# Reading the conditioning rows of a one-core decoder layer in two passes instead of four

## The chip, the cores and the metric

The kernel runs on one core of a Trainium2 chip. The time is the device time of one execution in microseconds (us); for the kernel before it is the median of three runs. The profile is of one more execution.

## The reference, cut to what matters

One decoder layer on 256 tokens of width 2048: a SwiGLU feed-forward of width 5632, a mixer (retention beside a sliding-window attention, gated and merged), a second such feed-forward, and a final norm. All three sub-layers are conditioned by one vector `c`:

```python
c_act = jax.nn.silu(c)
mod = (c_act @ w_ada[l] + b_ada[l]).reshape(b, N_MOD, D_MODEL)      # N_MOD = 9
h = modulate(rms_norm(x, norm_ffn1[l]), mod[:, 0], mod[:, 1])
x = x + 0.5 * mod[:, 2][:, None, :] * swiglu(h, w_ffn1_gu[l], w_ffn1_down[l])
...                                                                 # mod 3, 4, 5 and 6, 7, 8 likewise
```

So `w_ada`, 2048 by 9 x 2048 in float32 (151 MB), is read once, and each of its columns is multiplied by the same vector and summed.

## The kernel before, in words

**Matrix products.** Tokens lie in two halves of 128. A weight block of 512 rows by 512 columns (1 MB) is loaded by `load` (line 346) on the queue of SyncE (SP) into one of four buffers named `raw`. It is used in two pieces of 256 rows. `split` (line 365) makes of each piece a high part `wh`, rounded by ScalarE (ACT, line 369), and a low part `wl`, the rest, by VectorE (DVE, line 371); three buffers each hold them. `products` (line 349) then runs three matmuls for each of two blocks of 128 rows and two halves of tokens: high by high (line 356), high by low (357), low by high (359), in all 12 a piece, on TensorE (PE). Where the activations lie whole in memory, they are split too, by lines 404 and 405. The sums lie in four accumulator banks named `pa`. After a down product, line 622 multiplies a bank by the gate row, which frees the bank, and line 623 adds that to `x_sb`.

**Conditioning.** `w_ada` is handed over turned, so that one row of 2048 floats per partition holds what 128 outputs need; nine outputs of 2048 values make 144 such rows of 1 MB. `ada_load` (line 214) loads a row, on SP's queue. `ada_pass` (line 219) multiplies a stretch of it by `cact`, which holds silu(c) on all partitions, and sums it on DVE into one column of `sums`; the page shows it as CUSTOM_DVE_ANT_0, followed by a read of the accumulator. `ada_end` (line 233) adds up the columns of `sums`, adds the bias and multiplies by the norm's gain; for a gate, `gate_out` (line 287) sends it out to memory, from where it returns as a row.

**The opening** (until about 300 us) reads the 32 rows of outputs 0 and 1, which the first norm needs. It states its own pass counts, most of them in `group` (line 975): eight rows are read in one pass of 2048 columns each, the other 24 in two of 1024.

**The rows behind it**, 112 for seven outputs, are read beside the matrix products. `conditioning` (line 261) is a generator that makes one pass a step, four of 512 columns a row (`AQ`). Ahead of a pass it loads every row that is needed up to `pace["ahead"]` steps later. `tick` (line 313) is called behind each piece of 12 matmuls; it adds `pace["rate"]` to `pace["due"]` and takes a step for each whole one. Rates are written by hand for each stage (steps a tick): 1.0 and then 160/117 in the first feed-forward, 0.95, 0.25 and 0.95 before, in and behind the softmax of the mixer, and 64/150 in the second feed-forward, which begins at `due` = -5. At first in the first feed-forward and in the mixer a row takes one of the four `raw` buffers (ahead 1 and 2); later, and in the second feed-forward, rows have a ring of two buffers of their own (`slot` or `rows_x`), with ahead = `AQ`, so that the next row is asked for at the first step of a row.

**Order.** SP's order is that of the program. The order on the other engines is dealt by a planner that takes, of the instructions whose inputs are there by its own estimate, the one that the program has first; only the opening and the stretch around each norm are written out by hand (no rows are read in the latter).

Of the kernel before, what the change touches and what calls it, by code (L numbers as in the profile page):

```python
# [77 lines left out]
def layer_kernel(  # L78
# [41 lines left out]
    def nm(s):  # L120
        uid[0] += 1
        return f"{s}_{uid[0]}"
# [82 lines left out]

    modc = one.tile([P, 9, KD], F32, tag="modc", name="modc")

    AQ = 4

    def ada_load(m, k, w, loads=1):  # L210
        src = w_ada[(m * KD + k) * P : (m * KD + k + 1) * P, :]
        for i in range(loads):
            at = slice(i * D // loads, (i + 1) * D // loads)
            nc.sync.dma_start(w[:, at], src[:, at])

    def ada_pass(k, w, sums, q, passes=AQ):

        at = slice(q * D // passes, (q + 1) * D // passes)
        nc.vector.tensor_tensor_reduce(  # L219
            out=w[:, at],  # L220
            in0=w[:, at],
            in1=cact[:, at],
            scale=1.0,
            scalar=0.0,
            op0=ALU.mult,
            op1=ALU.add,
            accum_out=sums[:, k, q : q + 1],
        )

    def ada_sums():  # L230
        return two.tile([P, KD, AQ], F32, tag="sums", name=nm("sums"))

    def ada_end(m, ks, sums, i=None, passes=AQ):

        dest = modc[:, m, ks]
        if passes > 1:
            nc.vector.tensor_reduce(
                out=dest, in_=sums[:, ks, :passes], axis=AX.X, op=ALU.add
            )
            nc.vector.tensor_add(dest, dest, bcols[:, m, ks])  # L240
        else:
            nc.vector.tensor_add(dest, sums[:, ks, 0], bcols[:, m, ks])
        if i is not None:
            nc.vector.tensor_mul(dest, dest, gains[:, i, ks])
# [5 lines left out]
    def two_rows(both=None):  # L250

        both = slot() if both is None else both
        turn = [both[:, :D], both[:, D:]]

        def place():
            turn.append(turn.pop(0))
            return turn[-1]

        return place

    def conditioning(outputs, place, behind):


        tiles = [(m, k) for m, _, _ in outputs for k in range(KD)]
        held = {}
        step = 0
        for m, gain, row in outputs:
            sums = ada_sums()
            for k in range(KD):
                for q in range(AQ):  # L270
                    for i in range(step // AQ, min((step + pace["ahead"]) // AQ + 1, len(tiles))):
                        if i not in held:
                            held[i] = place()
                            ada_load(*tiles[i], held[i])
                    if behind is not None and step < 2 * AQ:
                        with tc.issue_after(behind.ins):
                            ada_pass(k, held[step // AQ], sums, q)
                    else:
                        ada_pass(k, held[step // AQ], sums, q)
                    step += 1  # L280
                    if k == KD - 1 and q == AQ - 1:
                        ada_end(m, slice(0, KD), sums, gain)
                        if row is not None:
                            gate_out(m, row)
                    yield
# [18 lines left out]
    pace = {"steps": iter(()), "rate": 0.0, "due": 0.0, "behind": None}  # L304

    def set_pace(outputs, halves, place, ahead):
        assert next(pace["steps"], None) is None
        pace["steps"] = conditioning(outputs, place, pace["behind"])
        pace["rate"] = len(outputs) * KD * AQ / halves
        pace["due"] = 0.0  # L310
        pace["ahead"] = ahead
# [386 lines left out]
    def ffn_up(held, w, tiles, first, bg=None, turned=(), ahead=None):  # L698
        for ci in range(first, DFF // CH):
            bg = bg or gemm(held, w, [ci * CH])[0]  # L700
            bu = gemm(held, w, [DFF + ci * CH], ahead=ahead)[0]
            swiglu_up(bg, bu, tiles, ci, by_dma=ci in turned)
            bg = ahead = None
# [407 lines left out]
    for g, ks in enumerate(groups):  # L1111
# [5 lines left out]
        due = 0 if final else 2 * len(groups[g + 1])  # L1117
# [34 lines left out]
    gate = gate_row()  # L1152
    tiles.append(slot())
    row_ring.append(two_rows())
    pace["rate"] = (192 - 32) / 117
    pace["ahead"] = AQ
    ffn_up(held, gu, tiles, EARLY, turned=range(EARLY, DFF // CH))
    gate_in = gate_load(gate, 2)
# [7 lines left out]
        nc.gpsimd.dma_start(x_d[t], x_sb[:, t, :])  # L1166
    soft = one.tile([P, NT * D], F32, tag="x", name="soft")
    planes_of = one.tile([P, D], F32, tag="row", name="planes_of")
    RATE_SOFT, RATE_AFTER = 0.25, 0.95
    row_ring.clear()  # L1170
    set_pace([(7, 2, None), (6, None, None), (5, None, 1.0)], 192 / 0.95, place_row, 2)

    def rows_beside():

# [331 lines left out]
    gate = gate_row()  # L1506
    tiles = [slot() for _ in range(3)]
    set_pace([(8, None, 0.5)], 150, two_rows(), AQ)
    pace["due"] = -5.0
    ffn_up(held, w_ffn2_gu[0], tiles, 0, head, range(DFF // CH), ahead)  # L1510
    gf = one.tile([P, KD * S], F32, tag="hh", name="gf")[:, :D]
    spare = one.tile([P, 2, KD * P], F32R, tag="hl", name="spare")
# [108 lines left out]
```

## Time and profile before

| | |
|---|---|
| median of three runs | 2370.66 us (2369.91 to 2371.54) |
| the profiled execution | 2372.7 us |
| its span | 2370.9 us |
| granted clock of PE | 0.999 |
| moved by DMA | 627.87 MB, mean 265 GB/s |
| stages | opening to 300 us, first feed-forward to about 780, mixer to about 1660, second feed-forward to the end |

The span is the time from the first to the last instruction of the program. In views of groups a row gives line, engine, operation, output and inputs, shape and count, then busy time and mean length, then the engine's idle time just ahead of it and what ended it. In a row of windows, the stretch and its length are followed by the busy time and the number of instructions of PE, PE's weight loads (PEld), DVE, ACT and POOL, then PE's granted clock, the share of DMA time and GB/s; for the instructions of a single line only that engine's busy time is given. A row of an engine's order in time has the start, the length, the instruction, and in brackets the idle time before it with what ended it.

### The profile page before, as it was taken

What the parts mean: (1) busy time and instruction counts of PE and PEld (TensorE: products, weight loads), DVE (VectorE), ACT (ScalarE), POOL (GpSimd) and SP (SyncE); (2) the same over time, 40 slices, a digit from 0 to 9 for tenths busy, and PEclk for the clock granted to TensorE, in tenths of its full rate; (3) what the DMA queues carried; (4) which work ended last, traced back from release to release, by engine and by line L of the source; (5) the groups of instructions that cost most, each with busy time, mean ns of one, the idle gap of its engine ahead of it and who ended that gap; (6) DMA issues with size and microseconds to landing.
All of it is one profiled execution on the core that took longest, in us unless ns stands there. A gap on an engine that the chain in (4) does not pass through costs nothing.

```text
span 2370.9 us, 28254 instructions
## 1 busy us (share of the span) xinstructions
PE 2343.7 (99%) x10431; PEld 1917.9 (81%) x10431; DVE 1702.8 (72%) x2624; ACT 1312.8 (55%) x1782; POOL 9.2 (0%) x21
## 2 busy tenths in 40 slices
PE   8999999999999999999999999999999999999998
PEld 5888888888788877778888888888888888888886
DVE  7887799778877768976777776677655555555656
ACT  6544456455546568775556564466455455455544
POOL 0000000000000000000000000000000000000000
PEclk9999999999999999999999999999999999999999
DMA  9977789998866898876778787755677777766553
GB/s 384 360 290 265 274 284 345 386 319 333 317 256 231 281 274 235 251 224 244 269 274 293 299 303 277 289 195 188 240 240 247 252 242 250 245 220 203 193 198 124
DMA packets 186316, 627.87 MB, mean 265 GB/s; under 512 B 108801, under 2 KB 109185, under 8 KB 115649
## 3 DMA queue, kind: packets, MB, share of 16 engines
q1 hardware_dynamic: 183682, 615.05, 74.7%
q0 software_dynamic: 1600, 9.83, 1.0%
q8 instruction: 82, 1.34, 0.2%
q10 hardware_dynamic: 896, 1.19, 0.1%
q14 instruction: 56, 0.46, 0.1%
HBM read 597.16 MB, written 4.22 MB: 254 GB/s over the span
## 4 chain that ended last, share of the span: by engine, by line
PE 55%; DVE 1%; issue 0%; ACT 0%; DVEq 0%
PE pa L359 18%; PE pa L356 18%; PE pa L357 18%; DVE wl L371 0%; PE ps L1316 0%; PE pd L1416 0%; PE pd L1415 0%; PE pd L1414 0%; PE pd L1401 0%; PE ps L832 0%; DVE home L465 0%; DVE soft L1303 0%; DVE t L622 0%; PE pd L1404 0%; DVE hl L465 0%
## 5 line engine op out<-in xcount | busy, mean ns | idle before, releaser
L369 ACT CAST wh<-raw 128x1024 fp32r<-128x1024 f32 x792 | 831.1, 1052 | 916.8 <-PE pa L357 887.6
L371 DVE TENSOR_TENSOR wl<-raw,wh 128x1024 fp32r<-128x1024 f32 x792 | 962.5, 1224 | 518.9 <-ACT wh L369 517.3
L356 PE MATMUL pa<-wh,hh 128*128 128x512 f32 x2184 | 854.9, 391 | 2.2 <-ACT wh L369 2.2
L357 PE MATMUL pa<-wh,hl 128*128 128x512 f32 x2184 | 851.2, 390 | 0.0
L359 PE MATMUL pa<-wl,hh 128*128 128x512 f32 x2184 | 774.5, 392 | 3.4 <-DVE wl L371 3.0
L359 PEld LDWEIGHTS pa<-wl,hh 128*128 128x128 f32 x2184 | 408.3, 188 | 93.9 <-DVE wl L371 8.8
L356 PEld LDWEIGHTS pa<-wh,hh 128*128 128x128 f32 x2184 | 410.1, 188 | 91.0 <-ACT wh L369 3.9
L357 PEld LDWEIGHTS pa<-wh,hl 128*128 128x128 f32 x2184 | 410.3, 188 | 84.5 <-issue 0.2
L357 PE MATMUL pa<-wh,a 128*128 128x512 f32 x944 | 366.5, 390 | 0.0
L356 PE MATMUL pa<-wh,a 128*128 128x512 f32 x944 | 350.0, 390 | 1.8 <-DVE t L622 1.8
L359 PE MATMUL pa<-wl,a 128*128 128x512 f32 x944 | 348.5, 390 | 1.0 <-DVE wl L371 1.0
L219 DVE CUSTOM_DVE_ANT_0 slot<-slot,cact 128x512 f32<-128x512 f32 (+2 forms) x272 | 209.8, 822 | 21.9 <-DMA slot<-in_w_ada_dram 21.9
L356 PEld LDWEIGHTS pa<-wh,a 128*128 128x128 f32 x944 | 177.1, 188 | 39.0 <-DVE t L622 2.2
L359 PEld LDWEIGHTS pa<-wl,a 128*128 128x128 f32 x944 | 177.2, 188 | 38.6 <-DVE wl L371 2.1
L357 PEld LDWEIGHTS pa<-wh,a 128*128 128x128 f32 x944 | 177.3, 188 | 37.8 <-DVE a L405 1.1
L530 ACT COPY slot<-back 128x512 uint16<-128x512 uint16 x140 | 93.4, 766 | 0.0
L219 DVE CUSTOM_DVE_ANT_0 raw<-raw,cact 128x512 f32<-128x512 f32 (+1 forms) x108 | 70.9, 708 | 23.1 <-DMA raw<-in_w_ada_dram 23.1
L219 DVE CUSTOM_DVE_ANT_0 rows_x<-rows_x,cact 128x512 f32<-128x512 f32 x124 | 78.8, 689 | 7.5 <-DMA rows_x<-in_w_ada_dram 7.3
L405 DVE TENSOR_TENSOR a<-slot,a 128x512 fp32r<-128x512 f32 x118 | 80.8, 686 | 0.3 <-ACT a L404 0.2
L514 ACT COPY flat<-t 128x512 uint16<-128x512 uint16 x128 | 72.7, 617 | 4.5 <-DVE t L1389 2.6
L404 ACT CAST a<-slot 128x512 fp32r<-128x512 f32 x118 | 72.5, 615 | 0.1
L219 DVE DVE_READ_ACCUMULATOR2_ANT sums<- 128x1 f32 x504 | 42.4, 84 | 0.0
(228 smaller groups left out, 1169.6 us busy)
## 6 DMA issues: line engine op xcount, KB each, us to landing
raw<-in_w_ffn_gu_dram SPq DMA_DIRECT2D x160, 1024.0 KB, 5.3
raw<-in_w_in_dram SPq DMA_DIRECT2D x104, 1024.0 KB, 6.0
raw<-in_w_ffn_down_dram SPq DMA_DIRECT2D x88, 1024.0 KB, 4.8
slot<-in_w_ada_dram SPq DMA_DIRECT2D x83, 1024.0 KB, 7.0
rows_x<-in_w_ada_dram SPq DMA_DIRECT2D x31, 1024.0 KB, 7.0
raw<-in_w_ada_dram SPq DMA_DIRECT2D x26, 1024.0 KB, 5.6
raw<-in_w_swa_branch_dram SPq DMA_DIRECT2D x16, 1024.0 KB, 5.8
raw<-in_w_ret_branch_dram SPq DMA_DIRECT2D x16, 1024.0 KB, 5.8
```

The lines of the kernel that those rows point to most:

```text
L219: nc.vector.tensor_tensor_reduce(out=w[:, at], in0=w[:, at], in1=cact[:, at], scale=1.0, scalar=0.0, op0=ALU.mult, op1=ALU.add, accum_out= ...
L356: nc.tensor.matmul(ps, ah[:, j, ts], wh[:, j, :], start=first, stop=False)
L357: nc.tensor.matmul(ps, al[:, j, ts], wh[:, j, :], start=False, stop=False)
L359: nc.tensor.matmul(ps, ah[:, j, ts], wl[:, j, :], start=False, stop=last).ins
L369: cast.append(nc.scalar.copy(hi, src).ins)
L371: low.append(nc.vector.tensor_sub(lo, src, hi.bitcast(F32)).ins)
L404: nc.scalar.copy(hi, v)
L405: nc.vector.tensor_sub(lo, v, hi.bitcast(F32))
L514: nc.scalar.copy(planes[:, i, :], words(src)[:, :, i])
L530: nc.scalar.copy(into[:, :, :, i], held["turned"][:, i])
```

## The change

`AQ` becomes 2: each of the 112 rows is read in two passes of 1024 columns, and `sums` has two columns a row. A step is now half a row, so all rates in steps a tick are halved, and so is the negative start of the second feed-forward. `ahead` is 2 steps in place of 4 where it follows `AQ`, 1 in place of 2 at the mixer's beginning, and stays 1 in the first feed-forward. The opening is as it was.

```diff
-    AQ = 4
+    AQ = 2
...
-    pace["rate"] = (192 - 32) / 117
+    pace["rate"] = (96 - 16) / 117
     pace["ahead"] = AQ
...
-    RATE_SOFT, RATE_AFTER = 0.25, 0.95
+    RATE_SOFT, RATE_AFTER = 0.125, 0.475
     row_ring.clear()
-    set_pace([(7, 2, None), (6, None, None), (5, None, 1.0)], 192 / 0.95, place_row, 2)
+    set_pace([(7, 2, None), (6, None, None), (5, None, 1.0)], 192 / 0.95, place_row, 1)
...
     set_pace([(8, None, 0.5)], 150, two_rows(), AQ)
-    pace["due"] = -5.0
+    pace["due"] = -2.5
```

The generator that takes the steps is not changed:

```python
            for k in range(KD):
                for q in range(AQ):
                    for i in range(step // AQ, min((step + pace["ahead"]) // AQ + 1, len(tiles))):
                        if i not in held:
                            held[i] = place()
                            ada_load(*tiles[i], held[i])
```

## The prediction

> **What bounds the kernel now.** I read the page's busy times first, then the same busy times by stage, then what TensorE (PE) waited for between 300 and 2100 us.
>
> ```profile
> span 2370.9 us, 28254 instructions
> PE 2343.7 (99%) x10431; PEld 1917.9 (81%) x10431; DVE 1702.8 (72%) x2624; ACT 1312.8 (55%) x1782; POOL 9.2 (0%) x21
> ```
>
> ```profile
> 0.00:30.00 30.00, 20.98 (x42) 9.65 (x43) 19.98 (x47) 15.02 (x30) 1.79 (x7) 1.00 0.95 368
> 30.00:300.00 270.00, 267.96 (x1188) 219.11 (x1187) 223.44 (x305) 132.60 (x162) 0.00 (x0) 1.00 0.83 310
> 2340.00:2400.00 60.00, 21.78 (x97) 17.70 (x95) 14.25 (x32) 4.93 (x12) 0.00 (x0) 0.95 0.09 35
> ```
>
> ```profile
> 300.00:470.00 170.00, 169.59 (x761) 139.45 (x760) 147.39 (x263) 98.51 (x127) 2.09 (x4) 1.00 0.96 336
> 470.00:680.00 210.00, 207.83 (x915) 171.04 (x914) 181.39 (x339) 110.47 (x136) 0.00 (x0) 1.00 0.88 324
> 680.00:840.00 160.00, 160.00 (x723) 132.69 (x722) 113.67 (x176) 94.69 (x133) 1.08 (x2) 1.00 0.71 248
> 840.00:1140.00 300.00, 296.92 (x1413) 237.34 (x1412) 225.38 (x378) 206.10 (x366) 0.53 (x1) 1.00 0.81 243
> 1140.00:1580.00 440.00, 440.00 (x1952) 364.52 (x1951) 321.80 (x543) 244.17 (x315) 2.10 (x4) 1.00 0.78 281
> 1580.00:1660.00 80.00, 78.64 (x358) 63.79 (x357) 59.85 (x87) 50.82 (x86) 0.00 (x0) 1.00 0.51 185
> 1660.00:2100.00 440.00, 440.00 (x1942) 364.11 (x1941) 249.80 (x315) 224.15 (x263) 1.04 (x2) 1.00 0.73 244
> ```
>
> ```profile
> PE pa L359 <- DVE wl L371: 4.7, 7, 1.6
> PE pa L356 <- DVE t L622: 1.8, 1, 1.8
> PE pa L356 <- ACT wh L369: 0.5, 1, 0.5
> ```
>
> In the windows the first number after the stretch's length is PE's busy time. PE stands still for 9.0 us in the first 30 us and for about 9.1 us after 2340 (the span ends at 2370.9, so 30.9 less 21.78). The change touches neither end: the opening states its own pass counts, and the last conditioning row is read before 2100. Between 30 and 300 PE is idle 2.0 us. From 300 to 2100, where the changed rows lie (the first few are read shortly before 300), it is idle 0.41 + 2.17 + 0 + 3.08 + 0 + 1.36 + 0 = **7.0 us**, and the three waits (in total, how often, the longest) sum to the same 7.0: 6.5 of them for DVE. That is the ceiling of any gain, 0.3% of the span, unless a matmul itself became quicker.
>
> Could a matmul become quicker with a lighter VectorE (DVE)? Two stretches without PE idle time and with different DVE loads answer that:
>
> ```profile
> 1380.00:1440.00 60.00, 60.00 (x266) 49.56 (x265) 43.37 (x73) 34.47 (x42) 0.00 (x0) 1.00 0.88 312
> 1860.00:1920.00 60.00, 60.00 (x266) 49.70 (x265) 35.80 (x50) 32.93 (x40) 0.00 (x0) 1.00 0.74 248
> ```
>
> With DVE at 43 or at 36 of 60 us PE starts the same 266 matmuls, one each 0.226 us: no. [...]
>
> **The change part by part.** It replaces 448 passes of 512 columns (112 rows by four) by 224 of 1024, with one accumulator read behind each.
>
> ```profile
> L219 DVE CUSTOM_DVE_ANT_0 slot<-slot,cact 128x512 f32<-128x512 f32 x220 | 139.2, 688 | 7.0 <-DMA slot<-in_w_ada_dram 7.0
> L219 DVE CUSTOM_DVE_ANT_0 rows_x<-rows_x,cact 128x512 f32<-128x512 f32 x124 | 78.8, 689 | 7.5 <-DMA rows_x<-in_w_ada_dram 7.3
> L219 DVE CUSTOM_DVE_ANT_0 raw<-raw,cact 128x512 f32<-128x512 f32 x104 | 66.0, 688 | 23.1 <-DMA raw<-in_w_ada_dram 23.1
> L219 DVE CUSTOM_DVE_ANT_0 slot<-slot,cact 128x1024 f32<-128x1024 f32 x44 | 52.2, 1224 | 12.7 <-DMA slot<-in_w_ada_dram 12.7
> L219 DVE DVE_READ_ACCUMULATOR2_ANT sums<- 128x1 f32 x504 | 42.4, 84 | 0.0
> ```
>
> 220 + 124 + 104 = 448. The recorded lengths (688 and 1224 ns) overlap, so I take starts from DVE's order in time: one row of now, and two passes of 1024, which the opening already uses.
>
> ```profile
> 344.89 0.69 DVE L219 CUSTOM_DVE_ANT_0 raw<-raw,cact 128x512 f32<-128x512 f32 x1 [2.07 <-DMA raw<-in_w_ada_dram]
> ...
> 347.35 1.22 DVE L371 TENSOR_TENSOR wl<-raw,wh 128x1024 fp32r<-128x1024 f32 x1
> ```
>
> ```profile
> 161.63 1.23 DVE L219 CUSTOM_DVE_ANT_0 slot<-slot,cact 128x1024 f32<-128x1024 f32 x1 [2.51 <-DMA slot<-in_w_ada_dram]
> ...
> 163.93 2.36 DVE L371 TENSOR_TENSOR wl<-raw,wh 128x1024 fp32r<-128x1024 f32 x2
> ```
>
> Four passes occupy DVE for 347.35 - 344.89 = 2.46 us, two wide ones for 163.93 - 161.63 = 2.30 us. So a row costs **0.16 us less**, 112 rows 17.9 us of DVE time, from 1702.8 to about 1685. The row also shows that the four passes of a row run in one burst when the row has landed, whatever ticks they were dealt to; two wide ones will do the same.
>
> [...]
>
> What of the 0.16 us is on PE's path? DVE makes the low halves of the weights (wl, line 371), three in flight:
>
> ```profile
> 702.14 1.05 ACT L369 CAST wh<-raw 128x1024 fp32r<-128x1024 f32 x1 [1.66 <-PE pa L357]
> ...
> 703.23 1.23 DVE L371 TENSOR_TENSOR wl<-raw,wh 128x1024 fp32r<-128x1024 f32 x1 [1.49 <-ACT wh L369]
> ```
>
> In the steady state ScalarE (ACT) is idle until PE gives back a weight buffer, and 2.3 us later (702.14 to 704.46) both halves are ready. Two other pieces of 12 matmuls, 2 x 12 x 0.226 = 5.4 us, lie ahead of that one on PE: a **cushion of 3.1 us**. A burst of 2.46 us in front of a split fits into it; so does one of 2.30. What PE gains by the shorter burst is nothing there. If the cushion is gone, every microsecond of a burst is on PE's path. Two places show it, and two smaller ones (the burst at 344.89 above, in front of an 0.2 us wait, and a like one 22 us later):
>
> ```profile
> 635.85 0.69 DVE L219 CUSTOM_DVE_ANT_0 slot<-slot,cact 128x512 f32<-128x512 f32 x1
> ...
> 638.90 0.69 DVE L622 TENSOR_TENSOR t<-pa,row 128x512 f32<-128x512 f32 x1
> ```
>
> ```profile
> 851.10 0.69 DVE L219 CUSTOM_DVE_ANT_0 raw<-raw,cact 128x512 f32<-128x512 f32 x1 [4.20 <-DMA raw<-in_w_ada_dram]
> ...
> 854.15 3.50 DVE L371 TENSOR_TENSOR wl<-raw,wh 128x1024 fp32r<-128x1024 f32 x3
> ```
>
> At 638.90 the last multiply that frees an accumulator bank (L622) stands behind a burst; that is the 1.8 us wait of PE. At 851.10 DVE sits 4.2 us before a row that has not landed, then runs the burst, and the split behind it is late: the 1.6 us wait. Four such places, 0.16 us each: **-0.6 us**.
>
> **The order.** A pass that can't be cut for 1.15 us (half of 2.30) instead of 0.61 can hold a split or a bank's release 0.53 us longer. DVE's order is dealt by the planner, not written out, so this can fall either way: between -0.5 and +0.5 us at each of the four places, up to 2.1 us either way. I take zero.
>
> **The loads.** The queue of SyncE (SP) follows the program's order. A step is now twice as long in ticks, and with the row ring ("ahead" = AQ) the next row is asked for at a row's first step, which comes one old step later; with ahead 2 turned into 1 it is asked for at the last step, again one old step later. With ahead 1 in the first feed-forward nothing moves. Each weight load that was behind a row load in that stretch goes ahead of it. SP waited there at times for a pass to give a row's buffer back, with a weight load next in line:
>
> ```profile
> SPq L346 <- DVE sums L219: 30.9, 15, 3.6
> ```
>
> PE's three waits hold none for a landing, so a shorter queue gains nothing on PE. What they could cost is a row that lands late under a planned burst, as at 851.10. The move is at most one old step, 1/0.95 ticks of 2.7 us = 2.9 us, at the one place where the cushion was gone: from -1.6 (that wait goes) to +2.9. I take zero, since DVE's burst moves with the row. No wait is added, and a row's result is needed only by the next norm, whose first use (line 850) comes 74 us behind the last pass of the first feed-forward:
>
> ```profile
> L219 DVE CUSTOM_DVE_ANT_0 slot<-slot,cact x156: 683/687/697, 375.8 to 676.3; 128x512 f32<-128x512 f32 x156
> ```
>
> ```profile
> L850 DVE TENSOR_SCALAR t<-pd,modc x10: 403/408/412, 750.4 to 776.3; 128x128 f32<-128x128 f32 x10
> ```
>
> **The sum.** 2372.7 us is the profiled execution's time, 1.8 over its span, and 2.0 over the median of the runs, 2370.66. 2372.7 - 0.6 = 2372.1, so on the median's footing **2370.1 us**. With the bounds: -0.6 - 2.1 - 1.6 = -4.3 and -0.6 + 2.1 + 2.9 = +4.4, that is 2366.4 to 2375.1.
>
> **The rivals.**
> 1. *The stalls go altogether.* The planner deals a fresh order in which the bursts at 635.85 and 851.10 miss the critical operations, and most of the 7.0 us disappears: 2370.7 - 5.5 = 2365.2 us. For it: two bursts stand directly before PE's two longest waits. Against: 1.36 us lie at 1580 to 1660, where no row is read, and part of the rest behind the softmax. Chance 0.08.
> 2. *Uncut passes hold the splits* (slower). The place is the dense stretch from 300 to 680, where DVE is busy 147 of 170 and 181 of 210 us. Of DVE's instructions there the passes and their reads are:
>
> ```profile
> 300.00:470.00 170.00, 47.44 (x150) 1.00 0.96 336
> 470.00:680.00 210.00, 68.70 (x216) 1.00 0.88 324
> ```
>
> 366 at eight a row are some 45 rows. Price 0.53 us (1.15 less 0.61) for each row that finds the cushion empty; it decides from ten such rows on (5.3 less the 0.6 gained is 4.7 us). If 15 of the 45 do, 8.0 - 0.6 on 2370.66 gives 2378.1 us. For it: 0.86 of DVE's time is taken there, so a delay isn't caught up quickly. Against: the cushion of 3.1 us is larger than a whole burst. A new order that brings fresh late rows like the one at 851.10, 1.6 us of PE each, would need three of them. Chance 0.20.
> 3. *The passes are not what they seem:* 1024 columns could run at another rate in the row ring than in the opening. The 44 opening passes of 1224 ns were made in the same kind of tile; I give it no chance of its own.
>
> **How the numbers follow.** Forecast 0.72, rival 1 0.08, rival 2 0.20. A measurement of this kernel can tell about 0.2%, 4.7 us, from no change; the runs shown spread over 1.6 us. The forecast lies within it, rival 1 below, rival 2 above: faster 0.08, same 0.72, slower 0.20. The range takes the forecast's bounds and reaches a little into both rivals, whose far halves stay out: 2365.8 to 2376.5.
>
> **What would show it.** Right: 224 fewer accumulator reads, DVE's busy time down by some 17 us (more by recorded lengths, as these overlap), the two wide passes of a row back to back 2.30 us long, PE's idle time between 300 and 2100 still near 7 us, and its pitch at 0.226. Wrong: new rows in PE's waits on line 371 or 622, above all from 300 to 680, or a longer idle time of DVE before line 219; then the order, not the work, made the time. If the pitch changes, the argument on the bound is wrong.

## The result and the profile after

The changed kernel takes 2377.11 us (median of 8 runs, 2374.56 to 2381.76); the kernel before, run beside it, 2370.30 us (8 runs, 2366.72 to 2377.0). The ratio is 1.0027, with a 95% interval of 1.0018 to 1.0035: 6.8 us slower, 0.27%. The forecast was 2370.1 us and the range ended at 2376.5, so the time lies outside. The profiled execution took 2379.06 us.

First the page's opening lines of the changed kernel, and its groups of line 219 on VectorE (DVE), where each row ends with the idle time of DVE ahead of the group:

```profile
span 2377.3 us, 27799 instructions
...
PE 2346.4 (99%) x10431; PEld 1915.7 (81%) x10431; DVE 1683.2 (71%) x2175; ACT 1312.4 (55%) x1781; POOL 9.2 (0%) x21
```

```profile
L219 DVE CUSTOM_DVE_ANT_0 slot<-slot,cact 128x1024 f32<-128x1024 f32 x154 | 182.4, 1219 | 20.2 <-DMA slot<-in_w_ada_dram 20.1
L219 DVE CUSTOM_DVE_ANT_0 rows_x<-rows_x,cact 128x1024 f32<-128x1024 f32 x62 | 73.4, 1221 | 11.1 <-DMA rows_x<-in_w_ada_dram 10.9
L219 DVE CUSTOM_DVE_ANT_0 raw<-raw,cact 128x1024 f32<-128x1024 f32 x56 | 66.5, 1222 | 31.9 <-DMA raw<-in_w_ada_dram 31.8
L219 DVE DVE_READ_ACCUMULATOR2_ANT sums<- 128x1 f32 x280 | 22.9, 82 | 0.0
```

The work went as reckoned: 504 - 280 = 224 accumulator reads are gone, the wide pass has the length of those of the opening (1219 to 1222 ns against 1224), and DVE is 19.6 us less busy. Its idle time ahead of the 112 rows rose, from 37.7 to 47.2 us, one of the signs that were named for a wrong forecast. TensorE's (PE's) busy time rose by 2.7 us with the same 10431 matmuls. Where its time went is seen by stages; the first number after a stretch's length is PE's busy time.

```profile
300.00:470.00 170.00, 168.74 (x754) 137.61 (x753) 144.17 (x189) 98.46 (x126) 2.10 (x4) 1.00 0.95 330
470.00:680.00 210.00, 207.24 (x910) 169.99 (x909) 174.64 (x225) 109.26 (x135) 0.00 (x0) 1.00 0.89 327
680.00:840.00 160.00, 160.00 (x723) 132.57 (x722) 113.58 (x150) 94.92 (x133) 1.09 (x2) 1.00 0.69 241
840.00:1140.00 300.00, 295.60 (x1403) 235.21 (x1402) 223.30 (x341) 205.29 (x364) 0.53 (x1) 1.00 0.79 243
1140.00:1580.00 440.00, 438.76 (x1941) 361.95 (x1940) 314.26 (x415) 240.94 (x311) 2.10 (x4) 1.00 0.77 280
1580.00:1660.00 80.00, 78.64 (x356) 63.75 (x355) 60.29 (x86) 51.32 (x82) 0.00 (x0) 1.00 0.54 192
1660.00:2100.00 440.00, 440.00 (x1945) 364.24 (x1944) 248.11 (x254) 225.00 (x268) 1.04 (x2) 1.00 0.72 243
```

```profile
PE pa L359 <- DVE wl L371: 7.3, 12, 1.7
PE pa L356 <- ACT wh L369: 1.3, 3, 0.5
PE pa L356 <- DVE t L622: 1.0, 1, 1.0
PE pa L357 <- DVE a L405: 0.9, 1, 0.9
PE pa L356 <- DVE t L682: 0.2, 1, 0.2
```

From 300 to 2100 PE is idle 11.0 us in place of 7.0: 1.26 instead of 0.41, then 2.76 instead of 2.17, 4.40 instead of 3.08, and 1.24 instead of none; the 1.36 from 1580 to 1660 stay. The waits for `wl` grew from 7 of 4.7 us to 12 of 7.3 us. Two of the old waits are gone, 1.59 us at 855 and 1.00 us at 1047; new ones between 527 and 1363 us come to 6.3 us. Idle time doesn't tell it all, since a matmul is recorded as 390 ns long while the next starts 227 ns later. So I also use **excess pitch**, worked out from the starts in the trace: between neighbouring matmuls of lines 356 to 359, whatever the distance of the starts has over 227 ns (by more than 8; distances near 454, where a record is missing, left out). Over the whole execution it is 23.7 us before and 29.9 us after, 6.2 more, for a span that is 6.4 us longer. By stage it is 5.0 and 7.7 from 300 to 680, 7.2 and 9.2 from 840 to 1140, 1.8 and 4.3 from 1140 to 1400.

Now a single place. This is DVE's order in the softmax of the mixer, before and after, around the same group of four heads. Line 1252 takes the maxima, 1255 their negatives, for which ScalarE's exponentials wait; 1265 needs all exponentials; 1303 are the four copies that put turned weights together.

```profile
946.06 0.68 DVE L219 CUSTOM_DVE_ANT_0 raw<-raw,cact 128x512 f32<-128x512 f32 x1
...
957.50 1.81 DVE L1252 TENSOR_REDUCE mx<-soft 128x4 f32<-128x1024 f32 x2
...
961.64 0.17 DVE L1255 TENSOR_SCALAR ng<-mx 128x8 f32<-128x8 f32 x1
961.77 1.59 DVE L1303 COPY soft<-a 128x768 uint16<-128x768 uint16 x3
...
966.01 0.17 DVE L1265 TENSOR_TENSOR sm<-sm,se 128x8 f32<-128x8 f32 x1 [2.09 <-ACT se L1257]
...
968.19 2.35 DVE L371 TENSOR_TENSOR wl<-raw,wh 128x1024 fp32r<-128x1024 f32 x2
```

```profile
956.33 1.80 DVE L1252 TENSOR_REDUCE mx<-soft 128x4 f32<-128x1024 f32 x2
959.47 1.23 DVE L219 CUSTOM_DVE_ANT_0 raw<-raw,cact 128x1024 f32<-128x1024 f32 x1 [1.35 <-DMA raw<-in_w_ada_dram]
...
964.12 0.16 DVE L1255 TENSOR_SCALAR ng<-mx 128x8 f32<-128x8 f32 x1
...
968.07 0.17 DVE L1265 TENSOR_TENSOR sm<-sm,se 128x8 f32<-128x8 f32 x1 [3.58 <-ACT soft L1261]
...
970.26 1.22 DVE L371 TENSOR_TENSOR wl<-raw,wh 128x1024 fp32r<-128x1024 f32 x1
971.39 2.06 DVE L1303 COPY soft<-a 128x768 uint16<-128x768 uint16 x4
973.35 2.33 DVE L371 TENSOR_TENSOR wl<-raw,wh 128x1024 fp32r<-128x1024 f32 x2
```

Before, the row's burst begins at 946.06, ahead of the maxima, and the copies fill the time in which the exponentials run. After, the burst stands between the maxima and their negatives: line 1255 comes at 964.12 instead of 961.64, though the maxima come 1.2 us sooner, DVE is then idle for 3.58 us, and the copies are behind that wait, in front of the splits. PE waits 0.36 us at 971.53 and 0.96 us at 974.60 for `wl`. A burst is not the only way to such a wait: the kernel before has one too, of 1.00 us at 1046.98, behind a group without a burst whose copies also stand behind the wait for the exponentials:

```profile
1040.44 0.17 DVE L1265 TENSOR_TENSOR sm<-sm,se 128x8 f32<-128x8 f32 x1 [1.80 <-ACT soft L1261]
...
1043.76 2.07 DVE L1303 COPY soft<-a 128x768 uint16<-128x768 uint16 x4
1045.73 2.33 DVE L371 TENSOR_TENSOR wl<-raw,wh 128x1024 fp32r<-128x1024 f32 x2
```

The row load itself, on SyncE's (SP's) queue, first before, then after:

```profile
940.05 0.33 SPq L214 DMA_DIRECT2D raw<-in_w_ada_dram  x1
```

```profile
953.44 0.33 SPq L214 DMA_DIRECT2D raw<-in_w_ada_dram  x1
```

It is 13.4 us later. In the softmax a step of the kernel before is 1/0.25 = 4 ticks of 2.7 us (12 matmuls at 0.227), so the quarter of a row by which the loads moved is 10.9 us there; PE's own delay up to that point, 2.4 us by the matmul of the same number, makes up most of the rest. From burst to burst it is some 51 us there, near twice the distance from one group of heads to the next, so that each row meets the groups at a like point: after, all four bursts of the softmax (910.00, 959.47, 1011.02 and 1061.78) stand between a group's maxima and their negatives, before none of them does.

### The profile page after: what moved, and what is told of

Read it like the earlier page. It is cut to its first block, busy times and chain, and to the rows that moved or that the text cites. A ratio compares the mean times of both kernels' runs of the same rounds, so it can differ in the third digit from the quotient of the medians.

```text
span 2377.3 us, 27799 instructions
## 1 busy us (share of the span) xinstructions
PE 2346.4 (99%) x10431; PEld 1915.7 (81%) x10431; DVE 1683.2 (71%) x2175; ACT 1312.4 (55%) x1781; POOL 9.2 (0%) x21
## 5 line engine op out<-in xcount | busy, mean ns | idle before, releaser
L371 DVE TENSOR_TENSOR wl<-raw,wh 128x1024 fp32r<-128x1024 f32 x792 | 961.5, 1222 | 528.4 <-ACT wh L369 525.4
L219 DVE CUSTOM_DVE_ANT_0 slot<-slot,cact 128x1024 f32<-128x1024 f32 (+1 forms) x162 | 200.7, 1272 | 22.3 <-DMA slot<-in_w_ada_dram 22.2
L219 DVE CUSTOM_DVE_ANT_0 raw<-raw,cact 128x1024 f32<-128x1024 f32 x56 | 66.5, 1222 | 31.9 <-DMA raw<-in_w_ada_dram 31.8
L219 DVE CUSTOM_DVE_ANT_0 rows_x<-rows_x,cact 128x1024 f32<-128x1024 f32 x62 | 73.4, 1221 | 11.1 <-DMA rows_x<-in_w_ada_dram 10.9
L1261 ACT ACTIVATE soft<-soft,ng 128x128 f32<-128x128 f32 (+1 forms) x64 | 28.2, 443 | 8.5 <-DVE ng L1255 8.4
```

Of the source, the lines that this page charges most:

```text
L219: nc.vector.tensor_tensor_reduce(out=w[:, at], in0=w[:, at], in1=cact[:, at], scale=1.0, scalar=0.0, op0=ALU.mult, op1=ALU.add, accum_out= ...
L371: low.append(nc.vector.tensor_sub(lo, src, hi.bitcast(F32)).ins)
L1261: nc.scalar.activation(of_t[:, i, :], of_t[:, i, :], AF.Exp, bias=ng[:, z : z + 1], accum_out=sm[:, z : z + 1],)
```

## The experiments

Two theories were stated first. **Grain:** a wide pass, 1.14 us from start to start where a narrow one has 0.61, holds the splits up. **Place:** the row loads come a quarter of a row later, and the bursts fall where they hurt. The rival to both: any new deal of the planner's order moves the time by some us, with no rule in it. Each ratio is against the kernel before on the same chip, with its 95% interval.

**1. The later loads alone.** Narrow passes at their old steps.

```diff
-    pace["ahead"] = AQ                      # in the first feed-forward and the mixer
+    pace["ahead"] = AQ - 1
...
-    set_pace([(7, 2, None), ...], 192 / 0.95, place_row, 2)
+    set_pace([(7, 2, None), ...], 192 / 0.95, place_row, 1)
...
-    set_pace([(8, None, 0.5)], 150, two_rows(), AQ)
+    set_pace([(8, None, 0.5)], 150, two_rows(), AQ - 1)
```

> Passes stay four of 512 columns at their old steps; only the row loads are asked for one quarter of a row later, as in the changed kernel. If the later loads made the 6.8 us (rows land later, DVE waits for them with splits behind), this is near 2377 us and DVE's idle time ahead of line 219 rises from 37.7 us for the 112 rows toward the changed kernel's 47.2. If the uncut wide passes made them, it stays near 2370 us. If any new deal of the planner's order moves the time by some us, it lies anywhere from 2368 to 2380.

Ratio **1.0033** (1.0021 to 1.0044): the whole loss, without a wide pass. PE's waits from 300 to 2100:

```profile
PE pa L359 <- DVE wl L371: 5.4, 9, 1.0
PE pa L356 <- DVE t L622: 1.8, 1, 1.8
PE pa L356 <- ACT wh L369: 1.4, 3, 0.5
PE pa L357 <- DVE a L405: 1.1, 1, 1.1
```

The wait for line 405 (at 527.55 us; 528.73 in the changed kernel) and those of 970.33, 973.42, 1025.16, 1302.06 and 1339.75 us are those of the changed kernel within 2 us; the kernel before has none of them. The expected sign did not come, though: DVE's idle time ahead of rows is 36.9 us, not more than the 37.7 before. What counts is where a burst stands, not how long DVE waits for the row.

**2. The wide passes alone.** Steps stay quarters; the passes are made at the second and the fourth, the loads stay.

```diff
-                    ada_pass(k, held[step // AQ], sums, q)
+                    for p, passes in [(q // 2, 2)] if q % 2 else []:
+                        ada_pass(k, held[step // AQ], sums, p, passes)
...
-                        ada_end(m, slice(0, KD), sums, gain)
+                        ada_end(m, slice(0, KD), sums, gain, 2)
```

> Two passes of 1024 columns a row, at the second and fourth quarter step as in the changed kernel, but the row loads stand where the kernel before has them. Uncut wide passes as the cause: near 2377 us, PE's excess pitch (starts of matmuls over 227 ns) near 30 us as in the changed kernel against 24 before. Later loads as the cause: near 2370 us. A mere new deal: anywhere from 2368 to 2380.

Ratio 1.0011 (1.0002 to 1.0020). PE's idle time from 300 to 2100 is 5.87 us, less than before, though the time is a little longer.

**3. Later loads, two narrow passes a step** (the same edit with `[(p, AQ) for p in (q - 1, q)]`, and the loads of 1).

> The changed kernel's steps and its later loads, but each step makes two passes of 512 instead of one of 1024, so that a split can go between them. Uncut passes as the cause: near 2370 us. Later loads as the cause: near 2377 us. A mere new deal: anywhere from 2368 to 2380.

Ratio **1.0034** (1.0022 to 1.0046).

**4. Old loads, two narrow passes a step.**

> Two passes of 512 together at the second and fourth quarter step, the loads as in the kernel before: the position of the passes alone. Uncut passes and later loads as causes both say near 2370 us; if it leaves 2370 by more than 3 us, the position in the program, or the new deal that it brings, moves the time by itself.

Ratio 1.0000 (0.9991 to 1.0009).

The six kernels make a table of loads by passes. With the later loads: 1.0033 (single), 1.0034 (pairs), 1.0027 (wide). With the old ones: 1, 1.0000, 1.0011. **Grain falls**; with the passes at their steps the place of the loads makes the loss, and the width some 0.1% at most, on whose sign the two rows differ. Most bursts run in one piece, narrow or wide, so there is little for a narrow pass to let through: before, another instruction stands inside 16 of 112 bursts (the one at 946.06 is among them), after, inside 3. PE's idle time from 900 to 1080 says the same: 3.92, 3.02 and 2.36 us with later loads (wide, single, pairs), 0, 1.00 and 0.96 with the old ones. The planner deals the order anew in each kernel, so place and order can't be told apart in a single one. But the pair of waits near 971 and 974 us stands in all three kernels with later loads and in none with the old ones, which speaks against mere chance.

Is later worse in itself, or is there only a best place?

**5. The changed kernel started a quarter of a row sooner.**

```diff
-        pace["due"] = 0.0
+        pace["due"] = 0.5
...
-    pace["due"] = -2.5
+    pace["due"] = -2.0
```

> The changed kernel, started a quarter of a row sooner in every stage (due 0.5 and -2.0), so that its row loads in the row rings stand at the ticks where the kernel before has them, with the wide passes. If the place of the loads in the program makes the 6.8 us, the time falls to 2370 to 2373 us and the waits of PE at about 527, 971 to 975, 1026, 1303 and 1340 us go. If the wide passes make it, it stays near 2377 us.

Ratio 1.0010 (1.0001 to 1.0018). The waits of the mixer that were named are gone, and the wait at 527 too; one of 2.2 us came at 652.29.

**6, 7, 8. The kernel before, all of it moved** by one quarter of a row later, two later, one sooner (the same edit, with -1, -2 and 1, and -6, -7 and -4 in the second feed-forward).

> The kernel before with everything, loads and narrow passes, one quarter of a row later (due -1 and -6): the loads stand where the changed kernel has them, the passes keep their distance to the loads. If the place of the loads decides, this is slow like the kernel with later loads alone (2377 to 2380 us) with waits of PE at the same places; if it is the distance from a load to its pass, it is near 2370 us.

> As the last, half a row later (due -2 and -7). If later is worse in itself, 2377 us or more. If it is a matter of where the row bursts fall among the stages' boundaries (a phase), the waits move to other places and the time can be anywhere from 2368 to 2380 us.

> The kernel before with everything a quarter of a row sooner (due 1 and -4). If later is worse in itself, at or below 2370 us. If it is a phase, anywhere from 2368 to 2380 us.

Ratios 1.0013 (1.0004 to 1.0023), 1.0059 (1.0045 to 1.0073), 1.0045 (1.0032 to 1.0057). It is **a phase**, the place of the bursts in a stage's work: sooner is slower too, and two quarters later is worse than one. The last two, at 2385.61 and 2382.94 us, lie outside even the wide range that was expected of a phase (2368 to 2380). The first came out less slow than expected, though its loads stand where those of the changed kernel do in the mixer. There it is like that kernel (excess pitch from 840 to 1400 us 13.2 us, against 13.4 there and 9.0 before), but from 300 to 680 it is the best of the kernels so far, 3.0 us against 5.0 before. It seems that a phase that suits one stage doesn't suit another.

**9. The mixer alone moved back.** The changed kernel with `pace["due"] = 0.5` behind the mixer's `set_pace`.

> The changed kernel with the mixer's rows alone moved a quarter of a row forward (due 0.5 there), the feed-forwards as changed. If the place of the rows against the work of each stage decides (phase), PE's excess pitch from 840 to 1400 us falls from 13.4 us to about 8, as in the wide kernel that was moved in every stage, and the waits at about 913, 971 to 975 and 1026 us go, while those at 527 and 373 us stay: about 1.001 to 1.0015 of the kernel before. If the wide passes in the softmax are to blame, the waits stay and the ratio is near 1.0027.

Ratio **0.9999** (0.9991 to 1.0008). PE in the two stretches of the mixer:

```profile
840.00:1140.00 300.00, 299.34 (x1426) 240.04 (x1425) 226.10 (x342) 207.62 (x366) 0.53 (x1) 1.00 0.82 246
1140.00:1580.00 440.00, 440.00 (x1952) 364.34 (x1951) 317.34 (x416) 243.98 (x314) 2.10 (x4) 1.00 0.77 280
```

It is idle 0.66 us there in place of 5.64, and excess pitch from 840 to 1400 us is 6.1 us, lower than the expected 8; the ratio, too, is lower than the expected 1.001 to 1.0015. The whole loss is won back by the place of the mixer's rows, with wide passes in the softmax. That isn't to say that they made all of it: from 300 to 680 excess pitch stays at 7.3 us (7.7 in the changed kernel, 5.0 before), and the mixer is now better than it was before.

**10. The first feed-forward alone moved** (the same behind its `set_pace`).

> The changed kernel with the rows of the first feed-forward alone moved a quarter of a row forward; the mixer as changed. By phase, excess pitch from 300 to 540 us falls from 5.5 us to about 1.8 and that of 600 to 680 rises from 2.2 to about 5, so that nearly nothing is won (ratio 1.002 to 1.0027), and the mixer's waits stay.

Ratio 1.0046 (1.0033 to 1.0060), slower than expected. Up to 757 us every engine and SP's queue have the same order as in 5, yet PE waits 1.59 us at 466.56 here and not there. Ahead of that, SP's queue stood at a transposing DMA (line 519), first here, then in 5:

```profile
443.55 14.90 SPq L519 DMA_TRANSPOSE back<-flat  x1
```

```profile
443.69 7.04 SPq L519 DMA_TRANSPOSE back<-flat  x1
```

The weight loads behind it came late, and ScalarE was idle 7.78 us for one. At the same place the issue took 11.32 us in 2 and 9.82 us in 7, and PE doesn't wait from 440 to 480 us in either, so a long issue is not enough for a wait. Why it took twice as long here as in 5 is open, and one profile can't show whether it did so in each execution. With one and the same order, excess pitch from 300 to 680 us is 6.7 us in 5 and 12.8 here: a difference of a few us in a stage between two profiles proves nothing by itself.

**11. The best place seen for each stage, put together.**

```diff
             set_pace(ROWS_FFN1, 32 * 192 // 32, place_row, 1)
+            pace["due"] = -1.0
...
+                    wide = m == 7
+                    for p, passes in [(q // 2, 2)] * (q % 2) if wide else [(q, AQ)]:
```

> The best place seen for each stage put together: first feed-forward with four narrow passes and everything a quarter of a row later, output 7 with two wide passes and the loads where the kernel before has them, the rest as before. If stages do not act on one another, excess pitch from 300 to 1140 us falls from about 12 us before to about 7, and the time to 2366 or 2367 us (0.998). If stages act on one another, or the place is not what decides, 2370 us or more.

2369.06 us, ratio **0.9986** (0.9977 to 0.9995): faster than both kernels, by less than expected. Excess pitch from 300 to 1140 us is 8.7 us (expected 7, before 12.9); from 1140 to 1400 it rose from 1.8 to 3.6, although the last wide pass is at 1122 us and the rows behind it are dealt as before, so it seems that a stage acts on the next.

**12. No rows in the softmax.**

```diff
-    RATE_SOFT, RATE_AFTER = 0.125, 0.475
+    RATE_SOFT, RATE_AFTER = 0.0, 0.53
```

> The changed kernel, but no row is read between the start and the end of the softmax (rate 0 there, 0.53 behind it in place of 0.475, so that all rows are read in time). If the row bursts between the maxima and the exponentials make the waits of the softmax, excess pitch from 900 to 1080 us falls from 7.2 us to 2 or less. What happens behind 1140 is open, since the rows stand elsewhere there. If the softmax's own chain makes the waits, they stay.

Ratio 1.0006 (0.9998 to 1.0015). From 900 to 1080 us, first the changed kernel, then this one:

```profile
900.00:1080.00 180.00, 176.08 (x857) 138.10 (x856) 145.96 (x231) 134.23 (x259) 0.00 (x1) 1.00 0.76 229
```

```profile
900.00:1080.00 180.00, 180.00 (x882) 143.39 (x882) 141.60 (x218) 136.44 (x263) 0.53 (x1) 1.00 0.80 224
```

No idle time in place of 3.92 us, and 1.7 us of excess pitch in place of 7.2, as expected: without bursts PE doesn't wait from 900 to 1080 us, so the softmax's chain alone doesn't make those waits. That a chain without a burst of its own can hold PE up in a kernel with bursts is seen at 1046.98 us before, where PE waits 1.00 us.

## Why the prediction was wrong

- **PE bounds the kernel, and a matmul doesn't get quicker:** right. PE is busy for 99% of the span in both profiles. From 1380 to 1440 PE starts 267 matmuls after and 266 before, from 1860 to 1920 266 in both.
- **0.16 us a row, 17.9 us of DVE time:** right (19.6 measured by busy time). That nothing of it reaches PE where the cushion holds was right too: from 680 to 840 and from 1660 to 2100 PE is idle 0 us before and after. Of the -0.6 us on the path only the wait for line 622 near 640 us can be checked: 1.76 to 1.77 us in the four narrow kernels with a burst just ahead of it (before, 1, 3, 4), 1.44 and 1.45 in the wide 2, 5 and 10, 1.05 in the changed kernel and 9. So a gain is there at that place, and it is lost among the new waits.
- **"Four such places" and a ceiling of 7 us:** the two larger places were read rightly (the third longest wait, 1.00 us at 1046.98, was left out), but the sum let the change act only there. The new order made other places: 527, 913, 971 to 975, 1026, 1303 and 1340 us had no wait before.
- **The order, zero between -2.1 and +2.1:** right in that the uncut pass doesn't decide (2, 3 and 4), and the distances that it was worked out from hold (passes of a burst start 0.61 us apart before, 1.14 after); the 0.1% that width may make, 2.4 us, is of the size of the bound.
- **The loads: the step that failed.** It put the move at "1/0.95 ticks of 2.7 us = 2.9 us", which is the rate outside the softmax. In the softmax the rate is 0.25 and a quarter of a row is 10.9 us; the load quoted above came 13.4 us later. And "I take zero, since DVE's burst moves with the row" was the wrong inference: the burst moves, but the splits, maxima and exponentials around it don't, so it meets other work. The bound was put at one place where the cushion was gone already, from -1.6 to +2.9 us. At that place the wait of 1.6 us did go; the loss came from elsewhere. What was measured is 4.0 us more idle time and 6.2 us more excess pitch, of which the mixer's rows make the larger part (4.4 us from 840 to 1400; 9 wins back 5.0 us of idle time and the time of the kernel before).
- **Rival 2** named the sign and gave 2378.1 us, near the 2377.1 measured, but by luck: its stretch, 300 to 680, holds 2.7 of the 6.2 us, and narrow passes with later loads lose as much. Nor is it rows that land late, the other way that it named: 1 loses as much with no more idle time ahead of its rows than before.
- In the first feed-forward the place of the loads fits in the six kernels of the table (excess pitch from 300 to 540 us 0.9 to 2.3 us with the old loads, 3.2 to 5.5 with the later ones), but not beyond: 6, with everything later, has 0.9, and 5 and 10, with the same order, have 1.8 and 5.3. So the part of that stage is not shown.

## What to carry to other kernels

A change of step size also moves whatever is counted in steps: work out the move in us for each stage by that stage's own rate (here 2.9 us outside the softmax and 10.9 in it), and look at what stands on the engine at the new place. With the same wide bursts, each run when its row lands, PE was idle for 0.66 us in the mixer at one place of the rows (9) and for 5.64 at another (the changed kernel), so where such work is dealt out beside a bound engine, its phase is a parameter of its own for each stage, to be tried apart from its size. A cushion read in the steady state, 3.1 us here, said nothing about a chain of maxima, exponentials and sums, behind which PE waited 1.00 us before and 0.36 and 0.96 after, nor about the end of a down product, where it waited 1.77 us for line 622 before. And a difference between two profiles in one stage is to be held against the difference between two profiles with the same order (6.7 and 12.8 us of excess pitch from 300 to 680 in 5 and 10).

## What the runs showed of the hardware that was not expected

The waits of PE cost more here than the idle time shown for them. At 971.53 us after, 0.36 us of idle time stand for starts 0.75 us apart, 0.52 over the pitch of 0.227; between the same two executions, 4.0 us more idle time stand beside 6.2 us more excess pitch. Also, runs of the kernel before spread wider than the first three showed: 2366.72 to 2377.0 us in eight.
